# Two transformer blocks on one core: the order of the first pieces, of a two-tile group, and of the last products

## The chip, the cores and the metric

The kernel runs on one core of one Trainium2 chip. The metric is the device time in microseconds (us). Before the change it is 2211.89 us, the median of 3 runs (2210.44 to 2212.3). A core has TensorE (PE in the profile; its weight loads are PEld), VectorE (DVE), ScalarE (ACT), GpSimd (POOL) and SyncE (SP, whose queue issues nearly all DMAs here).

## The reference

A layer stack of two blocks over x of 256 tokens by 2048 channels, batch 1, all in float32. The first block:

```
h    = rms_norm(x, mix_norm_g)
proj = h @ w_in                                   # q, kv, gate logits, conv input
attn = nsa_attention(q, kv, sigmoid(gates), ...)  # 16 heads: compressed, selected, window branch
conv = silu(layer_norm(depthwise31(a * sigmoid(gate))))   # 1024 channels
x    = x + concat([attn, conv]) @ w_out
h    = rms_norm(x, ffn_norm_g)
x    = x + (silu(g) * a) @ w_down                 # g, a: halves of depthwise3(h @ w_up)
x    = rms_norm(x, final_norm_g)
```

The second block takes that x and computes MLA attention and gated linear attention side by side, both from one `w_in`, then an output projection and a gated feed-forward part, each between adaptive norms:

```
x = x + gate_m * rms_norm(concat([mla, gla]) @ w_out, g_post_mix)
h = rms_norm(x, g_pre_ffn) * (1 + scale_f) + shift_f
f = (silu(h @ w_gate) * (h @ w_up)) @ w_down
return x + gate_f * rms_norm(f, g_post_ffn)       # the kernel's last lines
```

## The kernel before

**Products.** Every float32 operand is split into a high and a low part, and a product is three matmuls that add up in one PSUM bank: high by high, low by high, high by low. The weights lie in DRAM in the order in which they are used, as a list of groups (`make_plan`, `GROUPS`). A group has its output tiles of 128 columns and is cut into pieces of 1024 weight columns (`MCS`), 24 matmuls of 128x256 each; the last groups (`g2_0` to `g2_3`, the second feed-forward's down projection) take the tokens as the stationary side, 12 matmuls of 128x512 a piece, half for tokens 0 to 127 (`ps[0]`) and half for 128 to 255 (`ps[1]`). `run_group` writes the products of one group; `next_mc` keeps the preparation of pieces ahead: ACT copies the high part (`split_h`, tile `wh`), DVE subtracts to get the low part (`split_l`, tile `wl`), and `load_raw` starts the next transfer of raw weights (`raw`, three buffers; two pieces a transfer but for the first four) on SP's queue.

**Block 1, first stage.** The rows of x come as `XT` (channels on partitions). For each 128 channels `feed_h` makes the high part of x times the norm's gain (ACT, tile `X`), `feed_l` the low part (DVE). The norm itself isn't needed for the products: 1/rms, called `R`, multiplies the results when they leave PSUM. So the groups of `w_in` run before R is there, and only their evacuation waits for it. `first_gen` feeds the rows, squares them (ACT), adds the squares up (DVE, tile `ss`), sums them over the channels on PE (`sums`, a product with ones, `vecs`) and takes the root (ACT) and the reciprocal (DVE, `R`).

**Attention and conv.** The groups of `w_in` are, in order, c0, c1, kvc, c2, kk, gt, q0, q1, c3, vv, q2, q3 (c: conv inputs, four tiles; q: queries, two tiles). `att_driver` starts the heads when the compressed keys, the keys and the gates are there. A head ends on DVE with the reciprocal of its row sums (`rs`), the multiplication by the gates and the weights `Pc`. `conv_gen` does the depthwise conv: 31 taps for 8 tiles of 128 channels are 240 multiply-adds on DVE (`cacc<-upad,cat,cacc`, the first tap is ACT's); then the layer norm over channels: an add (`upad<-upad,cacc`), sums on PE (`ps<-upad,vecs`, first sums), subtract and square, sums on PE (second sums), 1/std, multiply (`cacc<-cacc,R`), silu on ACT (`upad<-cacc,cat`), split into `ch` (ACT) and `cl` (DVE), by halves of 4 tiles. The output projection is in groups oa, ob (they read attention's output `o`, four heads' pairs each) and oz (reads `ch`, `cl`). The flag `conv0` is set after the first half, `conv1` after the second.

**What sets the order.** Each engine runs its instructions in the order in which the program was written, and a small planner writes it: `Clock` keeps an estimated time for each engine; `tick`, called between products, lets side work (generators such as `first_gen`, `conv_gen`) proceed when it is due; a side with `low=True`, only `conv_gen`, goes last and stops while the estimated DVE time runs ahead of PE's by more than a limit. `later` defers an evacuation. `halves` cuts the first piece in two halves of 512 columns. So a change of one group's place or of one engine's load reorders much of what follows. `finish` (line 1997) is the end of the kernel: for each half of the tokens the last square, the root, the gain, and four scalings with the residual, each followed by a DMA of 256 KB to the output.

The diagnostic line: all operations are issued by one helper, line 306, so the profile's rows are told apart by the tiles that they write and read.

Of the kernel before, what the change touches and what calls it, by code (L numbers as in the profile page):

```python
# [13 lines left out]
F32 = mybir.dt.float32  # L14
# [9 lines left out]
T = 256  # L24
# [16 lines left out]
def make_plan():  # L41
# [15 lines left out]
    conv(0)  # L57
    conv(1)
# [4 lines left out]
    q(0)  # L63
# [83 lines left out]
WARM = 8  # L147
SQ = 1
AHEAD = 2
SKIP = 48  # L150
# [223 lines left out]
class Kern:  # L374
    def __init__(self, nc, tc, a, dump=None, stop=None):
# [11 lines left out]
        self.hl = {}  # L387
# [60 lines left out]
    def load_raw(self, n):  # L448
        while self.loaded < min(n, MCS[self.last_mc]["tile"] + 1, self.used + RAW):
# [3 lines left out]
            self.sy.dma_start(raw[:, :L], bass.AP(tensor=w.tensor, offset=w.offset + off, ap=[[L, 128], [1, L]]))  # L453
# [3 lines left out]
    def split_h(self, i):  # L457
        m = MCS[i]
        h = self.wp.tile([128, 1024 + 64], F32R, name="wh", bufs=LA + 1)[:, OFF:]
        for a, b in halves(i, m["len"]):  # L460
            self.act(h[:, a:b], self.raws[m["tile"]][:, m["o"] + a:m["o"] + b], AF.Copy)
        self.hl[i] = h

    def split_l(self, i):
        m = MCS[i]
        n, h = m["len"], self.hl[i]
        l = self.wp.tile([128, 1024 + 64], F32R, name="wl", bufs=LA)[:, OFF:]
        for a, b in halves(i, n):
            self.tt(l[:, a:b], self.raws[m["tile"]][:, m["o"] + a:m["o"] + b], h[:, a:b].bitcast(F32), OP.subtract)
        self.hl[i] = (h, l)  # L470
        if i == len(MCS) - 1 or MCS[i + 1]["tile"] != m["tile"]:
            self.raws.pop(m["tile"])
            self.used = m["tile"] + 1
            self.load_raw(self.used + RAW)

# [76 lines left out]
    def run_group(self, g):  # L552
# [5 lines left out]
        src = self.src  # L558
# [10 lines left out]
        kl = len(g["ks"]) - 1  # L569
# [3 lines left out]
        for mi in g["mcs"]:  # L573
# [6 lines left out]
            h, l = self.next_mc(mi)  # L580
            t["PE"] = max(t["PE"], self.l_end.pop(mi))
            for u in range(nt if g["mode"] == "w" else 2):
                o = ps[u][:min(n, 128)] if g["mode"] == "w" else ps[u][:, :n]
                for q, k in enumerate(m["ks"]):
                    xh, xl = src(k, N)
                    if g["mode"] == "w":
                        c = slice(q * n + u * 128, q * n + u * 128 + min(n, 128))
                        p = ((h[:, c], xh), (h[:, c], xl), (l[:, c], xh))
                    else:
                        c, ts = slice(q * n, q * n + n), slice(u * 128, u * 128 + 128)  # L590
                        p = ((xh[:, ts], h[:, c]), (xl[:, ts], h[:, c]), (xh[:, ts], l[:, c]))
                    for i, (a, b) in enumerate(p):
                        self.mm(o[:, :b.shape[1]], a, b, k == 0 and i == 0, k == kl and i == 2)
# [3 lines left out]
            if mi != g["mcs"][-1]:  # L597
                self.tick()
# [1434 lines left out]
```

## Time and profile before

| | |
|---|---|
| median of 3 runs | 2211.89 us (2210.44 to 2212.3) |
| profiled execution, its own time | 2210.07 us |
| span of the profiled execution | 2208.1 us |
| mean granted clock of TensorE over the span | 0.996 of full speed |
| PE busy | 2176.1 us, 99% |
| DVE busy | 1695.1 us, 77% |
| ACT busy | 1187.3 us, 54% |
| chain that ended last | PE 92%, DVE 4%, ACT 2% |

The profile is of one execution. Busy time says how full an engine was over the whole span; the chain says what the end waited for, step by step. A row of the timeline gives the start in us from the span's start, the duration, the engine, the line, the operation with output and inputs, the shapes, and, in brackets, how long the engine had stood idle before it and on whose result. A row of a stretch gives busy time and count for PE, PEld, DVE, ACT and POOL, the granted clock (1.00 is 2.4 GHz, 0.50 is 1.2 GHz), the DMA share and the bytes moved per time.

### The profile page before, as it was taken

The page shows a single profiled execution, that of the slowest core. Times are in us where ns is not written, and L with a number is a line of the kernel's source. Part 1 is how long each engine was busy: PE and PEld are TensorE (multiplying, and loading weights), DVE is VectorE, ACT ScalarE, POOL GpSimd, SP SyncE. Part 2 cuts the span into 40 slices and gives each one's busy share as a digit, 9 for nine tenths or more (in the row PEclk, how much of TensorE's full clock was granted, in tenths as well). Part 3 has the DMA queues.
Part 4 walks back from the last instruction along what each step waited for, and adds up shares of the span by engine and source line. Part 5 has one row for each costly group of instructions (what it writes and reads, how often), then busy time and mean ns, then how long its engine had stood idle before and what let it go on. Part 6 is the DMA issues. An engine that isn't in the chain of part 4 may idle for free.

```text
span 2208.1 us, 42338 instructions
## 1 busy us (share of the span) xinstructions
PE 2176.1 (99%) x17486; PEld 2083.7 (94%) x17486; DVE 1695.1 (77%) x2632; ACT 1187.3 (54%) x1826; POOL 4.9 (0%) x16
## 2 busy tenths in 40 slices
PE   8999999999999999999999999999999999999997
PEld 8998889999999999999999889989998999899986
DVE  7998988999988799998879876678666665554455
ACT  5447786655553355555556664566444444444443
POOL 0000000000000000000000000000000000000000
PEclk9999999999999999999999999999999999999999
DMA  6544325688888887887756643546766765555553
GB/s 248 191 170 157 119 96 193 242 301 312 306 299 313 304 305 293 308 298 292 265 206 226 225 144 137 209 152 211 251 248 240 253 250 201 198 186 177 192 193 131
DMA packets 89089, 499.22 MB, mean 226 GB/s; under 512 B 9904, under 2 KB 12352, under 8 KB 42432
## 3 DMA queue, kind: packets, MB, share of 16 engines
q1 hardware_dynamic: 88896, 496.51, 62.8%
q8 instruction: 137, 2.24, 0.4%
q14 instruction: 56, 0.46, 0.1%
HBM read 494.35 MB, written 2.12 MB: 225 GB/s over the span
## 4 chain that ended last, share of the span: by engine, by line
PE 92%; DVE 4%; ACT 2%; issue 1%; DMA 1%; SPq 0%; DVEq 0%; ACTq 0%
PE ps L306 92%; DVE wl L306 1%; DMA raw<-in_wst_dram 1%; DVE cacc L306 1%; ACT wh L306 0%; DVE og L306 0%; ACT P L306 0%; DVE ss L306 0%; DVE XT L306 0%; DVE blk L306 0%; ACT L306 0%; ACT X L306 0%; DVE R L306 0%; DVE X L306 0%; DVE P L306 0%
## 5 line engine op out<-in xcount | busy, mean ns | idle before, releaser
L306 PE MATMUL ps<-X,wh 128*128 128x256 f32 (+1 forms) x7680 | 1333.1, 278 | 3.3 <-ACT X L306 2.6
L306 ACT ACTIVATE wh<-raw 128x1024 fp32r<-128x1024 f32 (+2 forms) x741 | 782.7, 1058 | 817.5 <-PE ps L306 770.8
L306 DVE TENSOR_TENSOR wl<-raw,wh 128x1024 fp32r<-128x1024 f32 (+2 forms) x741 | 897.8, 1215 | 404.8 <-PE ps L306 348.1
L306 PEld LDWEIGHTS ps<-X,wh 128*128 128x128 f32 x7680 | 1160.7, 188 | 11.9 <-issue 5.8
L306 PE MATMUL ps<-X,wl 128*128 128x256 f32 (+1 forms) x3840 | 1059.9, 276 | 3.5 <-DVE wl L306 3.5
L306 PEld LDWEIGHTS ps<-X,wl 128*128 128x128 f32 x3840 | 721.7, 188 | 4.5 <-DVE wl L306 4.5
L306 DVE SCALAR_TENSOR_TENSOR ac<-wa,cs,ac 128x512 f32<-128x512 f32 x360 | 269.4, 748 | 8.3 <-DMA wa<-in_wada_dram 2.0
L306 PE MATMUL ps<-hid,wh 128*128 128x256 f32 x1408 | 241.4, 276 | 0.0
L306 PE MATMUL ps<-wh,hid 128*128 128x512 f32 x704 | 216.7, 388 | 0.0
L306 PEld LDWEIGHTS ps<-hid,wh 128*128 128x128 f32 x1408 | 211.8, 188 | 1.2 <-issue 1.2
L306 PE MATMUL ps<-hid,wl 128*128 128x256 f32 x704 | 193.7, 275 | 0.0
L306 PEld LDWEIGHTS ps<-wh,hid 128*128 128x128 f32 x704 | 131.8, 188 | 27.4 <-issue 0.2
L306 PE MATMUL ps<-wl,hid 128*128 128x512 f32 x352 | 136.6, 388 | 0.0
L306 PEld LDWEIGHTS ps<-hid,wl 128*128 128x128 f32 x704 | 132.2, 188 | 0.0
L306 DVE SCALAR_TENSOR_TENSOR cacc<-upad,cat,cacc 128x256 f32<-128x256 f32 x240 | 99.6, 476 | 0.3 <-ACT cacc L306 0.2
L306 PEld LDWEIGHTS ps<-wl,hid 128*128 128x128 f32 x352 | 66.1, 188 | 13.6
L306 DVE SCALAR_TENSOR_TENSOR y<-vt,fv,y 128x256 f32<-128x256 f32 x176 | 73.3, 478 | 0.0
L306 PE MATMUL ps<-wh,X 128*128 128x512 f32 x192 | 61.1, 399 | 0.0
L306 ACT ACTIVATE y<-ps,fv 128x256 f32<-128x256 f32 x84 | 49.3, 587 | 0.0
L306 PE MATMUL ps<-o,wh 128*128 128x256 f32 x256 | 46.8, 283 | 1.2 <-ACT o L306 1.1
L306 ACT ACT_TABLE_LOAD x30 | 38.5, 1283 | 10.9 <-DMA XT<-in_x_dram 5.4
L306 PEld LDWEIGHTS ps<-wh,X 128*128 128x128 f32 x192 | 35.4, 188 | 6.7
(319 smaller groups left out, 1747.9 us busy)
## 6 DMA issues: line engine op xcount, KB each, us to landing
raw<-in_wst_dram SPq DMA_DIRECT2D x363, 1024.0 KB, 4.9
wa<-in_wada_dram SPq DMA_DIRECT2D x176, 512.0 KB, 6.2
wa<-in_wada_dram SPq DMA_DIRECT2D x32, 256.0 KB, 5.5
raw<-in_wst_dram SPq DMA_DIRECT2D x4, 768.0 KB, 4.3
raw<-in_wst_dram SPq DMA_DIRECT2D x4, 512.0 KB, 5.9
B<-dtab SPq DMA_DIRECT2D x8, 256.0 KB, 5.1
out_dram<-og SPq DMA_DIRECT2D x8, 256.0 KB, 2.8
XT<-in_x_dram SPq DMA_DIRECT2D x3, 512.0 KB, 7.1
```

The source lines that it names most:

```text
L306: return f(*x, **k)
```

## The change

1. **Group order.** q0, a two-tile group, comes second, behind c0, instead of behind gt.
2. **First piece.** `first_piece` does piece 0 in two halves of 512 columns, each with one row of x (`feed_h`, the half of `wh`, `feed_l`, the half of `wl`), and `run_group` writes its products row by row over all tiles instead of tile by tile. The first raw tile is loaded in two halves from ACT's queue, the next ones stay on SP's; XT's first two rows come in two transfers. One warm-up product fewer (`WARM` 7).
3. **Rows and squares.** `first_gen` feeds the rows of piece c when piece c-1 is prepared, and does all squares after all rows.
4. **Table.** An activation on a constant column (`kc[:, 4:5]`) is put ahead of the first use of XT, so that ACT's table is loaded there.
5. **End.** Of the last group's last three pieces (`TAIL`), half 0's products come first and half 1's after them (`held`, `products`). `last_add` takes each half in with two adds of 256 columns and squares of them, `last_scale` does the scalings; half 0's are done while half 1's products run, but for two.

```diff
@@ make_plan
     conv(0)
+    q(0)
     conv(1)
...
     add("gt", "w_in", [np.array([2560 + h * 3 + br for h in HORD for br in range(3)])], K16, 8)
-    q(0)
     q(1)
@@ constants
-WARM = 8
-SQ = 1
+WARM = 7
 AHEAD = 2
+TAIL = 3
@@ load_raw
-            self.sy.dma_start(raw[:, :L], bass.AP(tensor=w.tensor, offset=w.offset + off, ap=[[L, 128], [1, L]]))
+            for a, b in halves(self.loaded, L):
+                (eng or self.sy).dma_start(raw[:, a:b], bass.AP(tensor=w.tensor, offset=w.offset + off + a, ap=[[L, 128], [1, b - a]]))
@@ new
+    def first_piece(self, g):
+        h = self.wp.tile([128, 1024 + 64], F32R, name="wh", bufs=LA + 1)[:, OFF:]
+        l = self.wp.tile([128, 1024 + 64], F32R, name="wl", bufs=LA)[:, OFF:]
+        self.hl[0], raw = (h, l), self.raws[0]
+        for k, (a, b) in enumerate(halves(0, MCS[0]["len"])):
+            self.feed_h((k,), g)
+            self.act(h[:, a:b], raw[:, a:b], AF.Copy)
+            self.feed_l((k,), g)
+            self.tt(l[:, a:b], raw[:, a:b], h[:, a:b].bitcast(F32), OP.subtract)
+        self.prepped = 1
@@ run_group
+        ends = len(g["mcs"]) - (TAIL if g is GROUPS[-1] else 0)
...
+            us = range(nb)
+            if n_mc >= ends:
+                held.append((m, hl))
+                us = (0,)
+            order = [(u, q) for q in range(len(m["ks"])) for u in us] if mi == 0 else [(u, q) for u in us for q in range(len(m["ks"]))]
+            for u, q in order:
+                self.products(g, ps[u], u, m, q, hl, N)
...
+        if held:
+            self.later(lambda: self.last_add(0, ps[0]), False)
+            for m, hl in held:
+                for q in range(len(m["ks"])):
+                    self.products(g, ps[1], 1, m, q, hl, N)
+                    self.tick()
+            self.later(lambda: self.last_add(1, ps[1]), False)
+            self.flush()
+            return
@@ block1_setup
-        for n, (c0, c1) in enumerate(((0, 2), (2, 4), (4, 8))):
+        self.load_raw(1, nc.scalar)
+        for n, (c0, c1) in enumerate(((0, 1), (1, 2), (2, 4), (4, 8))):
             self.load_x(c0, c1)
-            self.load_raw(n + 1)
+            self.load_raw(n)
         self.load_x(8, 12)
+        self.act(self.kc[:, 4:5], self.eps, AF.Identity)
         g = lambda k: self.ca("mix_g", k)
-        self.feed_raw(range(2), g)
+        self.h_end[0] = self.clock.run(lambda: self.first_piece(g), 0.0)[1]
@@ first_gen
-        for c in range(1, 8 + SQ):
-            if c < 8:
-                self.feed_raw(range(2 * c, 2 * c + 2), g)
+        for c in range(1, 8):
+            while self.cur == "c0" and (self.prepped < c or self.emitted < c - AHEAD):
+                yield
+            self.feed_raw(range(2 * c, 2 * c + 2), g)
...
+        yield
+        ss4 = self.early.tile([128, 2, T], F32, name="ss4", tag="g1")
+        for c in range(8):
...
+            yield
@@ new, in place of finish
+    def last_add(self, tt, ps):
+        f = self.f[:, tt, 1536:]
+        q = self.f2.tile([128, 512], F32, name="q", tag="u")
+        for e in range(2):
+            c = slice(256 * e, 256 * e + 256)
+            self.tt(f[:, c], ps[:, c], f[:, c], OP.add)
+            self.act(q[:, c], f[:, c], AF.Square, accum_out=self.ssq[:, tt, 3 + e:4 + e])
+        self.last_f = self.f2.tile([128, 512], F32, name="lf", bufs=2), *getattr(self, "last_f", ())
+        self.tt(self.last_f[0], f, self.gpb[1][:, 1], OP.mult)
+        if tt:
+            self.last_scale(0, (2, 3), self.last_f[1])
+        R = self.rp.tile([128, T], F32, name="sd")[:, :1]
+        self.v.tensor_reduce(R, self.ssq[:, tt], axis=AX, op=OP.add)
+        self.act(R, R, AF.Sqrt, scale=1.0 / D, bias=self.eps)
+        r = self.rt[tt] = self.f2.tile([128, 1], F32, name="r", bufs=2)
+        self.v.reciprocal(r, R)
+        self.last_scale(tt, range(4) if tt else (0, 1), self.last_f[0])
```

The order of the instructions follows from the planner, so it is shown at three places.

VectorE at the start of the program, before (`X<-XT,cat,X` is the low part of a row, `wl` that of a piece, `ss<-ss,sq` the add of a square):

```order
L306 SCALAR_TENSOR_TENSOR X<-XT,cat,X 128x256 x2
L306 TENSOR_TENSOR wl<-raw,wh 128x512 x2
L306 SCALAR_TENSOR_TENSOR X<-XT,cat,X 128x256 x4
L306 TENSOR_TENSOR ss_154<-ss_154,sq_177 128x512
L306 TENSOR_TENSOR wl<-raw,wh 128x1024
L306 SCALAR_TENSOR_TENSOR X<-XT,cat,X 128x256 x2
L306 TENSOR_TENSOR ss_154<-ss_154,sq_204 128x512
L306 SCALAR_TENSOR_TENSOR X<-XT,cat,X 128x256 x2
L306 TENSOR_TENSOR ss_154<-ss_154,sq_229 128x512
L306 TENSOR_TENSOR wl<-raw,wh 128x1024 x2
```

The same place after the change:

```order
L306 SCALAR_TENSOR_TENSOR X<-XT,cat,X 128x256
L306 TENSOR_TENSOR wl<-raw,wh 128x512
L306 SCALAR_TENSOR_TENSOR X<-XT,cat,X 128x256
L306 TENSOR_TENSOR wl<-raw,wh 128x512
L306 SCALAR_TENSOR_TENSOR X<-XT,cat,X 128x256 x4
L306 TENSOR_TENSOR wl<-raw,wh 128x1024
L306 SCALAR_TENSOR_TENSOR X<-XT,cat,X 128x256 x2
L306 TENSOR_TENSOR wl<-raw,wh 128x1024 x2
L306 SCALAR_TENSOR_TENSOR X<-XT,cat,X 128x256 x4
L306 TENSOR_TENSOR wl<-raw,wh 128x1024 x2
L306 SCALAR_TENSOR_TENSOR X<-XT,cat,X 128x256 x2
L306 TENSOR_TENSOR wl<-raw,wh 128x1024
```

The adds of squares have gone from between the rows; they come after the last row, from the 17th instruction row on. On PE the sums of `ss` stand behind 240 products of `X` instead of 174.

VectorE at the end of attention, before, from the last head's `rs` on:

```order
L306 RECIPROCAL rs<-sm 128x6
L306 TENSOR_TENSOR rs<-rs,Gt 128x6
L306 SCALAR_TENSOR_TENSOR Pc_1829<-sc,rs,cat 128x16 x2
L306 TENSOR_TENSOR upad<-upad,cacc_91 128x2x256
L306 TENSOR_TENSOR o<-ps,o 128x256
L306 TENSOR_TENSOR wl<-raw,wh 128x1024
L306 TENSOR_TENSOR XT<-ps,XT 128x256 x4
L306 TENSOR_TENSOR cacc_90<-cacc_90,sd 128x1024
L306 TENSOR_TENSOR cacc_91<-cacc_91,sd 128x1024
```

The same place after the change:

```order
L306 RECIPROCAL rs<-sm 128x6
L306 TENSOR_TENSOR rs<-rs,Gt 128x6
L306 SCALAR_TENSOR_TENSOR Pc_1945<-sc,rs,cat 128x16 x2
L306 TENSOR_TENSOR XT<-ps,XT 128x256 x2
L306 SCALAR_TENSOR_TENSOR cacc_91<-upad,cat,cacc_91 128x256 x16
L306 TENSOR_TENSOR o<-ps,o 128x256
L306 TENSOR_TENSOR upad<-upad,cacc_91 128x2x256
L306 TENSOR_TENSOR wl<-raw,wh 128x1024
L306 TENSOR_TENSOR cacc_90<-cacc_90,sd 128x1024
```

Sixteen multiply-adds of the conv (`cacc_91<-upad,cat,cacc_91`) and two adds to XT now stand between the last `Pc` and the conv's last add (`upad<-upad,cacc_91`); there was nothing between them. The subtractions `cacc_90<-cacc_90,sd` belong to the norm behind the first sums.

TensorE at the conv's first sums (`ps<-upad,vecs`), before (`PT` are attention's last products, `o` the output projection):

```order
L306 MATMUL ps<-vecs,P_3721 128x128 x2
L306 MATMUL ps<-upad,vecs 128x256 x2
L306 MATMUL ps<-PT,vz 64x256 x2
L306 MATMUL ps<-PT,V 64x256 x2
L306 MATMUL ps<-PT,V 64x128 x2
L306 MATMUL ps<-PT,V 64x256 x2
L306 MATMUL ps<-PT,V 64x128 x2
L306 MATMUL ps<-o,wh 128x256 x2
L306 MATMUL ps<-o,wl 128x256
```

The same place after the change:

```order
L306 MATMUL ps<-PT,V 64x128 x2
L306 MATMUL ps<-PT,V 64x256 x2
L306 MATMUL ps<-PT,V 64x128 x2
L306 MATMUL ps<-o,wh 128x256 x2
L306 MATMUL ps<-o,wl 128x256
L306 MATMUL ps<-o,wh 128x256 x2
L306 MATMUL ps<-o,wl 128x256
L306 MATMUL ps<-upad,vecs 128x256 x2
L306 MATMUL ps<-o,wh 128x256 x2
L306 MATMUL ps<-o,wl 128x256
```

The first sums have moved behind the last products of attention and six of the output projection. Between the first and the second sums of the conv stood 18 products of `o`, and 174 between the second sums and the first product of oz (`ps<-ch,wh`); now it is 138 and 48.

## Rows read from the trace of the kernel before

**Rows 1.** The page, busy time of each engine and the chain that ended last
```profile
PE 2176.1 (99%) x17486; PEld 2083.7 (94%) x17486; DVE 1695.1 (77%) x2632; ACT 1187.3 (54%) x1826; POOL 4.9 (0%) x16
...
PE 92%; DVE 4%; ACT 2%; issue 1%; DMA 1%; SPq 0%; DVEq 0%; ACTq 0%
```

**Rows 2.** Timeline of PE at the start (start us, duration, instruction; wait before it)
```profile
8.13 0.51 PE L306 MATMUL ps<-X,wh 128*128 128x256 f32 x2 [0.73 <-ACT wh L306]
...
14.52 0.39 PE L306 MATMUL ps<-X,wl 128*128 128x256 f32 x1 [2.39 <-DVE wl L306]
...
18.45 0.39 PE L306 MATMUL ps<-X,wl 128*128 128x256 f32 x1 [0.90 <-DVE wl L306]
...
34.23 0.70 PE L306 MATMUL ps<-ss,vecs 128*128 128x256 f32 x2 [1.46 <-DVE ss L306]
```

**Rows 3.** Timeline of DVE in the last 20 us
```profile
2188.34 1.23 DVE L306 TENSOR_TENSOR wl<-raw,wh 128x1024 fp32r<-128x1024 f32 x1 [1.49 <-PE ps L306]
...
2196.44 0.69 DVE L306 TENSOR_TENSOR og<-ps,og 128x512 f32<-128x512 f32 x1 [0.67 <-PE ps L306]
...
2197.11 0.68 DVE L306 TENSOR_TENSOR og<-og,wa 128x512 f32<-128x512 f32 x1
...
2197.90 2.74 DVE L306 SCALAR_TENSOR_TENSOR og<-og,sd,XT 128x512 f32<-128x512 f32 x4
...
2200.56 0.15 DVE L306 TENSOR_REDUCE sd<-ssq 128x1 f32<-128x4 f32 x1
...
2201.41 2.74 DVE L306 SCALAR_TENSOR_TENSOR og<-og,sd,XT 128x512 f32<-128x512 f32 x4
```

**Rows 4.** Busy time by stretch, R to the conv's end, and oz
```profile
36.00:310.40 274.40, 271.34 (x2166) 250.64 (x2165) 250.16 (x643) 169.51 (x390) 0.57 (x2) 0.99 0.43 154
343.50:391.00 47.50, 47.14 (x416) 46.94 (x414) 41.31 (x70) 32.83 (x54) 0.14 (x2) 1.00 0.60 212
```

**Rows 5.** Timeline of PE, the conv's sums and the first oz product
```profile
313.91 1.03 PE L306 MATMUL ps<-upad,vecs 128*128 128x256 f32 x4
...
321.50 1.13 PE L306 MATMUL ps<-upad,vecs 128*128 128x256 f32 x4 [0.66 <-DVE upad L306]
...
343.51 0.28 PE L306 MATMUL ps<-ch,wh 128*128 128x256 f32 x1
```

**Rows 6.** Timeline of ACT and DVE at the start
```profile
5.36 1.28 ACT L306 ACT_TABLE_LOAD   x1 [5.36 <-DMA XT<-in_x_dram]
...
35.97 1.75 DVE L306 RECIPROCAL R<-sd 128x256 f32<-128x256 f32 x1 [0.20 <-ACT sd L306]
```

**Rows 7.** The page's groups, the conv's multiply-adds
```profile
L306 DVE SCALAR_TENSOR_TENSOR cacc<-upad,cat,cacc 128x256 f32<-128x256 f32 x240 | 99.6, 476 | 0.3 <-ACT cacc L306 0.2
```

**Rows 8.** Timeline of DVE at the end of attention
```profile
309.59 0.19 DVE L306 RECIPROCAL rs<-sm 128x6 f32<-128x6 f32 x1 [2.85 <-ACT sc L306]
...
310.38 0.68 DVE L306 TENSOR_TENSOR upad<-upad,cacc 128x512 f32<-128x512 f32 x1
...
313.34 1.41 DVE L306 TENSOR_TENSOR XT<-ps,XT 128x256 f32<-128x256 f32 x4
```

**Rows 9.** Timeline of ACT and DVE, from the conv's norm to its output
```profile
331.15 1.99 ACT L306 ACTIVATE wh<-raw 128x1024 fp32r<-128x1024 f32 x2
...
333.05 1.05 ACT L306 ACTIVATE ch<-upad 128x1024 fp32r<-128x1024 f32 x1
...
334.13 1.23 DVE L306 TENSOR_TENSOR cl<-upad,ch 128x1024 fp32r<-128x1024 f32 x1
...
335.27 1.22 DVE L306 TENSOR_TENSOR cacc<-cacc,R 128x1024 f32<-128x1024 f32 x1
...
336.52 2.08 ACT L306 ACTIVATE upad<-cacc,cat 128x256 f32<-128x256 f32 x4 [2.43 <-DVE cacc L306]
```

**Rows 10.** Busy time by stretch around the fall of the granted clock
```profile
1457.00:1460.30 3.30, 1.27 (x6) 0.68 (x4) 2.76 (x7) 1.17 (x3) 0.00 (x0) 1.00 0.74 293
1460.30:1467.10 6.80, 6.01 (x23) 5.25 (x24) 5.89 (x11) 4.11 (x9) 0.00 (x0) 0.50 0.00 0
```

More of the change, by code (lines that the diff above doesn't have):

```diff
@@ L459, in split_h @@
         h = self.wp.tile([128, 1024 + 64], F32R, name="wh", bufs=LA + 1)[:, OFF:]
-        for a, b in halves(i, m["len"]):
-            self.act(h[:, a:b], self.raws[m["tile"]][:, m["o"] + a:m["o"] + b], AF.Copy)
+        self.act(h[:, :m["len"]], self.raws[m["tile"]][:, m["o"]:m["o"] + m["len"]], AF.Copy)
         self.hl[i] = h
@@ L466, in split_l @@
         n, h = m["len"], self.hl[i]
[L467 to L470, printed above, removed]
+        if i:
+            l = self.wp.tile([128, 1024 + 64], F32R, name="wl", bufs=LA)[:, OFF:]
+            self.tt(l[:, :n], self.raws[m["tile"]][:, m["o"]:m["o"] + n], h[:, :n].bitcast(F32), OP.subtract)
+            self.hl[i] = (h, l)
         if i == len(MCS) - 1 or MCS[i + 1]["tile"] != m["tile"]:
@@ L579, in run_group @@
                 self.idle()
-            h, l = self.next_mc(mi)
+            hl = self.next_mc(mi)
             t["PE"] = max(t["PE"], self.l_end.pop(mi))
[L582 to L593, printed above, removed]
-                    if q % GRAN == GRAN - 1 and (u, k) != (nb - 1, m["ks"][-1]):
-                        self.tick()
+            us = range(nb)
[5 more added lines that the diff above has]
+                self.products(g, ps[u], u, m, q, hl, N)
+                if q % GRAN == GRAN - 1 and (u, m["ks"][q]) != (nb - 1, m["ks"][-1]):
+                    self.tick()
             self.emitted += 1
@@ L605, in run_group, with products @@
         self.tick()
+    def products(self, g, bank, u, m, q, hl, N):
+        n, (h, l), k = g["n"], hl, m["ks"][q]
+        xh, xl = self.src(k, N)
+        if g["mode"] == "w":
+            o = bank[:min(n, 128)]
+            c = slice(q * n + u * 128, q * n + u * 128 + min(n, 128))
+            p = ((h[:, c], xh), (h[:, c], xl), (l[:, c], xh))
+        else:
+            o = bank[:, :n]
+            c, ts = slice(q * n, q * n + n), slice(u * 128, u * 128 + 128)
+            p = ((xh[:, ts], h[:, c]), (xl[:, ts], h[:, c]), (xh[:, ts], l[:, c]))
+        for i, (a, b) in enumerate(p):
+            self.mm(o[:, :b.shape[1]], a, b, k == 0 and i == 0, k == len(g["ks"]) - 1 and i == 2)
     def xsrc(self, k, N=T):
@@ new lines, in last_scale @@
+    def last_scale(self, tt, js, last):
+        x = self.XT.rearrange("p (c a) t -> p c (a t)", a=2)
+        for j in js:
+            o = self.f[:, tt, 512 * j:512 * j + 512]
+            f = last if j == 3 else o
+            self.stt(o.rearrange("p (c n) -> p c n", c=2), f.rearrange("p (c n) -> p c n", c=2), self.rt[tt],
+                     x[:, 2 * j:2 * j + 2, 256 * tt:256 * tt + 256], OP.mult, OP.add)
+            self.sy.dma_start(self.a["out"][128 * tt:128 * tt + 128, 512 * j:512 * j + 512], o)
```

43 lines of the change are left out of this document (10 added, 33 removed).

## The prediction

> **What bounds the kernel now.** I read the busy shares and the chain first: TensorE is busy 99% of the span and 92% of the chain that ended last is its products [rows 1]. So an edit pays only where PE stands still, and the next view is the idle time at PE's own rows. At the beginning it stands 0.73 us for the first weights, 2.39 and 0.90 us for `wl` of the second and third pieces and 1.46 us for the sum of squares `ss` [rows 2]: 5.5 us in all. At the end the span of 2208.1 runs on for 11.7 us after the last product, on VectorE, whose last add starts at 2196.44 [rows 3]. In between, the table by stage (columns: stretch, PE, PEld, DVE, ACT, POOL busy, granted clock, DMA share, GB/s) shows that from 36 to 310 us PE is full but DVE works 250.2 of 274.4 us as well [rows 4]: attention and the depthwise conv of block 1 live there. Their end is due on PE: the conv's first sums start at 313.91 with no wait, its second ones at 321.50 after 0.66 us, and the oz products that read the conv's output at 343.51 with no wait [rows 5]. That is a schedule with nothing to spare, and it hangs on R, which is ready from 35.97 + 1.75 us [rows 6]. The change moves R.
>
> **The beginning.** One piece is 24 products. A stretch of nothing but products gives 47.14 / 416 = 0.113 us each [rows 4], so 2.72 us a piece.
> Gains: piece 0 is split and multiplied row by row, with one warm-up product fewer and the table load moved ahead of the XT transfer (1.28 us, which now ends the wait for XT [rows 6]). First product about 0.9 us earlier (the most is the 1.28). `wl` of the second piece stood behind four row subtractions and a square's add on DVE; in the new order it stands behind the rows but no add, and its raw tile lands no sooner. I take 1.1 of the 2.39 us and all of the 0.90 us [rows 2], and charge 0.7 for a new wait at the fifth piece, whose `wl` now stands behind four rows. Net 2.2 us; the bounds are 0 and 0.9 + 3.3 = 4.2.
> Cost: all squares now come after all rows, so the sums of `ss` stand on PE behind 240 products instead of 174. 66 x 0.113 = 7.5 us, less the 2.2 gained, less the 1.46 us wait for `ss` that goes [rows 2]: R is 3.8 us later (bounds 1.8 and 7.5). No evacuation of the first groups can run before R, so glu, attention and conv all start that much later. q0 second costs two banks and no product; what it could give is an earlier start of attention, below.
>
> **From R to the conv's sums.** On DVE the work between R and the conv's last add is the same but for some 0.8 us (the same instructions, with five more). If DVE idles as much as before (274.4 - 250.2 = 24.2 us [rows 4]), the last add of the conv comes 3.8 + 0.8 = 4.6 us later, and the first sums at 313.91 + 4.6 = 318.5 [rows 5]. The order gives a second reading: 16 of the conv's multiply-adds, of 99.6 / 240 = 0.415 us [rows 7], now stand after the last head's `rs`, where none stood. With `rs` at 309.59 as before, 0.8 to the end of Pc (310.38), 0.7 for two XT adds (1.41 for four), 16 x 0.415 = 6.6, 0.35 for an o add (as one XT add), 0.68 for the conv's add [rows 8], and 0.2 to PE's start, the sums stand at 319.0; `rs` itself could be later by R's delay. The two agree; I take 319.0, with bounds 313.9 (attention, freed by the early q0, cuts the idling by as much as R is late) and 322 (R 7.5 us late). PE reaches that point earlier than before and waits, which is where the gain of the beginning is spent: below it counts for nothing.
> From there PE's order decides. Before, 18 o products stood between the two sums; now 138. The second sums come at 319.0 + 1.03 + 138 x 0.113 = 335.7 instead of 321.50 [rows 5]. From them to `ch` of the first half took 12.6 us (321.50 to 333.05 + 1.05), in which two `wh` of 1.99 us stood ahead of `ch`; these have gone from that place, so 10.6 [rows 9]: oz starts at 346.3 rather than 343.51. The cover is gone too: only 48 o products (5.4 us) are left behind the second sums, 335.7 + 1.1 + 5.4 = 342.2, so PE waits 4.1 us. Then comes a wait that was hidden before: the second half of the conv. After `ch` at 346.3, `cl` 1.23, the product with R 1.22, four silu 2.08, a `wh` 1.0, `ch` 1.05 and `cl` 1.2 [rows 9] end at 354.0 (rounded), where before the second piece could go on at 343.51 + 2.72 = 346.2. That is 7.7 us with what is rounded; I take **7.6**, bounds 0 and 11. Behind the waiting oz product stand all later ones, and PE is 99% busy after it [rows 4], so it isn't won back.
>
> **TensorE's clock.** In one place of this trace PE stood 2 us beside thin work (1.27 of 3.30 us busy) and the granted clock was then 0.50, the 1.2 GHz level, for 6.80 us [rows 10]; after the 2.39 us wait at the start it didn't fall. Waits of 4 us in front of oz lie beyond both. A fall of the length seen costs 6.01 us of busy time at half rate, 3.0; the shortest that I could defend is nothing. I take 1.7, near the middle, once.
> The Trainium skill (TensorE: Matmul & The Clock Gate, section "HAM oscillation — how this bites in real kernels") says that a loop whose waits re-throttle the array pays again at each wait. This trace bears it out at one of the two places; with a payment at each of the two long waits before oz the sum would be 1.7 us higher, which is the third rival.
>
> **The end.** The last three pieces do half 0's products first, so half 0 is complete 18 products of 512 columns before the end (18 x 2 x 0.113 = 4.1 us), and half 1 at the same time as now. Before, the last add stood at 2196.44, a multiply of 0.68 follows, then four scalings of 2.74 for half 0, and half 1's four from 2201.41 to 2204.15 [rows 3]. After: two adds of half width 0.7 from 2196.44, the multiply 0.68, half 0's last two scalings 1.37, then reduction, root and reciprocal 0.85 (2201.41 less 2200.56 before), four scalings 2.74: 2202.8. That is **-1.4** (bounds -2.5 and 0). `wl` of the last piece, which waited for its buffer 1.49 us [rows 3], gets it when the piece four earlier is done, 8.2 us before the end, and is ready 6.8 before it; half 0 of the last piece wants it 5.0 before it (4.1 + 4 products): nothing lost.
>
> **Sum.** On the profiled execution of 2210.1: +7.6 - 1.4 + 1.7 = 2218.0. The median of the runs stands 1.8 above that execution: **2219.8 us**.
>
> **Rivals.**
> *Attention catches up.* The early q0 lets the heads start when gt is done instead of 10.9 us later (four pieces), so DVE idles less than its 24.2 us [rows 4]. For it: those us of idling are there; against: the conv is given low priority and the order still leaves 16 of it to the end. With 3.5 us less idling the sums come at 315.5, oz loses 4.1 instead of 7.6, no clock fall: 2210.1 + 4.1 - 1.4 + 1.8 = 2214.6.
> *The other side: the conv is in time.* If DVE idles some 7 us less, the conv's last add is there by 311 and PE never waits at the sums. PE keeps 2.2 + 1.46 = 3.7 of the beginning and 1.4 of the end: 2210.1 - 5.1 + 1.8 = 2206.8. It decides from a last add of about 311 on; the 16 multiply-adds after `rs` would have to start before 304, against which the order speaks.
> *The clock falls at both waits.* 2219.8 + 1.7, and as much again if a fall stretches the conv's chain: 2221.5 to 2223.2.
> *The beginning doesn't gain.* The first raw tile is issued from ACT's queue, behind nothing, but its halves share the transfers with XT. If piece 0 is no earlier, R is 2.2 later, the sums at 321: 2222.
>
> **How the numbers follow.** Forecast 0.44 (own range 2217 to 2222.5), attention catches up 0.24, the conv in time 0.14, the clock falls twice 0.12, no gain at the start 0.06. What a measurement can tell from no change is 0.2%, 4.4 us: below 2207.5 or above 2216.3. Faster: 0.12 of the 0.14. Same: 0.02 of it, 0.20 of the catching up and 0.02 of the forecast, 0.24. Slower: the rest, 0.64. The range from 2208.5 to 2224.5 leaves out some 0.12 below and 0.05 above.
>
> **What would show it.** In the profile of the changed kernel: the first product near 7.2 and the sums of `ss` near 38.0 with no wait; R near 39.8; the conv's first sums at 318.5 to 320 with a wait of 3 us or more in front; the second ones with no wait; oz with a wait of about 4 us on `ch` and another, of some 4 in parts, on the second half; the granted clock at 0.50 for a few us right there; the last scaling 1.4 us nearer to PE's last product. A conv sum before 314, or an oz without a wait, proves the forecast wrong, and a time under 2210 does so too.

## The result and the profile after

The changed kernel takes 2223.53 us (median of 4 runs, 2222.85 to 2225.03) against 2211.40 of the kernel before beside it: ratio 1.0058, 95% interval 1.0046 to 1.0071. It is slower by 12 us, on the side that was forecast (+7.9), 4 us more than the likeliest case and 1.0 above that case's own range (2217 to 2222.5). The profiled execution took 2224.05.

The page of the changed kernel, busy time and the chain that ended last:

```profile
PE 2181.7 (98%) x17484; PEld 2088.2 (94%) x17484; DVE 1697.4 (76%) x2634; ACT 1187.5 (53%) x1829; POOL 4.9 (0%) x16
...
PE 90%; DVE 4%; ACT 4%; DMA 1%; issue 1%; DVEq 0%; ACTq 0%
```

PE's share of the chain fell from 92 to 90% and ACT's rose from 2 to 4%, while DVE's stayed at 4% [rows 1]: on the path to the end PE now waits for ACT more often.

PE and DVE at the start of the changed kernel, and the stretch in which the clock fell (columns of the stretch: length, PE, PEld, DVE, ACT, POOL busy, granted clock, DMA share, GB/s):

```profile
6.07 0.50 PE L306 MATMUL ps<-X,wh 128*128 128x256 f32 x2
...
10.76 0.50 PE L306 MATMUL ps<-X,wh 128*128 128x256 f32 x2 [1.18 <-ACT wh L306]
...
13.55 0.39 PE L306 MATMUL ps<-X,wl 128*128 128x256 f32 x1 [2.28 <-DVE wl L306]
...
40.23 0.70 PE L306 MATMUL ps<-ss,vecs 128*128 128x256 f32 x2
...
41.97 1.75 DVE L306 RECIPROCAL R<-sd 128x256 f32<-128x256 f32 x1 [0.20 <-ACT sd L306]
```
```profile
14.80:18.10 3.30, 3.30 (x18) 3.30 (x17) 1.95 (x2) 1.06 (x1) 0.00 (x0) 0.50 0.89 344
```

The first product comes 2.1 us earlier than before (8.13 [rows 2]), but PE then stands 1.18 us for the second piece's `wh` and 2.28 us for its `wl`, and runs at the 1.2 GHz level for 3.3 us. The sums of `ss` stand at 40.23 instead of 34.23 and R at 41.97 instead of 35.97 [rows 6]: 6.0 us late, in these two executions.

PE in the middle of the changed kernel: a product of attention, the conv's first and second sums, the two halves of the conv in front of oz, and the sums behind oz:

```profile
278.40 0.69 PE L306 MATMUL ps<-PT,vz 128*64 128x256 f32 x1 [3.19 <-ACT PT L306]
...
326.76 1.10 PE L306 MATMUL ps<-upad,vecs 128*128 128x256 f32 x4 [2.66 <-DVE upad L306]
...
343.36 1.03 PE L306 MATMUL ps<-upad,vecs 128*128 128x256 f32 x4
...
354.19 0.58 PE L306 MATMUL ps<-ch,wh 128*128 128x256 f32 x1 [4.34 <-ACT ch L306]
...
355.45 0.58 PE L306 MATMUL ps<-cl,wh 128*128 128x256 f32 x1 [0.68 <-DVE cl L306]
...
360.59 0.38 PE L306 MATMUL ps<-ch,wh 128*128 128x256 f32 x1 [0.36 <-ACT ch L306]
...
361.85 0.39 PE L306 MATMUL ps<-cl,wh 128*128 128x256 f32 x1 [0.88 <-DVE cl L306]
...
406.89 0.70 PE L306 MATMUL ps<-ss,vecs 128*128 128x256 f32 x2 [0.63 <-DVE ss L306]
```

The first sums wait 2.66 us and are 12.9 us later than before, the first oz product waits 4.34 us and is 10.7 us later [rows 5], and the sums behind oz, at 391.27 before, are 15.6 us later. From there nothing more is lost: PE's last product ends 15.7 us later than before (2212.1 against 2196.4), and the end gives 1.5 us of it back. DVE at the end of attention shows the queue that the forecast read from the order:

```profile
317.80 0.18 DVE L306 RECIPROCAL rs<-sm 128x6 f32<-128x6 f32 x1
...
319.27 6.42 DVE L306 SCALAR_TENSOR_TENSOR cacc<-upad,cat,cacc 128x256 f32<-128x256 f32 x16
...
325.94 0.68 DVE L306 TENSOR_TENSOR upad<-upad,cacc 128x512 f32<-128x512 f32 x1
```

Sixteen multiply-adds take 6.42 us between the last head and the conv's last add; before, 0.8 us lay between `rs` and that add [rows 8]. But `rs` itself is 8.2 us late.

The clock around the two long waits of the changed kernel:

```profile
275.00:278.40 3.40, 0.21 (x1) 0.00 (x1) 2.31 (x15) 2.88 (x12) 0.00 (x0) 0.88 0.00 0
278.40:282.00 3.60, 3.60 (x18) 2.32 (x18) 0.67 (x5) 3.08 (x14) 0.00 (x0) 0.50 0.00 0
...
350.00:354.20 4.20, 0.01 (x1) 0.01 (x1) 1.63 (x4) 3.13 (x5) 0.00 (x0) 0.82 0.76 250
354.20:358.00 3.80, 3.12 (x13) 2.83 (x14) 3.47 (x3) 1.43 (x3) 0.00 (x0) 0.50 0.03 6
```

In front of both PE did almost nothing (0.21 of 3.40 us, 0.01 of 4.20), and behind both the granted clock is 0.50, as at [rows 10]. Behind the 2.66 us wait at 326.76 it stayed at 1.00.

A ledger makes the kernels comparable. From stretches of 2 us between 0 and 420, idle is the stretch less PE's busy time, and half rate is the busy time times (1 - granted clock):

| kernel | median us | ratio to before, 95% | idle | half rate | sum |
|---|---|---|---|---|---|
| before | 2211 | | 13.2 | 1.7 | 14.9 |
| changed | 2223.5 | 1.0046 to 1.0071 | 23.3 | 8.7 | 32.0 |
| e1 squares early | 2212.4 | 0.9999 to 1.0016 | 13.7 | 6.6 | 20.3 |
| e2 q0 second only | 2222.8 | 1.0043 to 1.0069 | 22.0 | 7.7 | 29.7 |
| e3 q0 back | 2212.8 | 0.9999 to 1.0017 | 13.5 | 6.7 | 20.2 |
| e4 end only | 2209.1 | 0.9984 to 1.0002 | 10.9 | 4.7 | 15.6 |
| e5 changed, limit 1.5 | 2217.7 | 1.0018 to 1.0041 | 16.6 | 8.3 | 24.9 |
| e6 before, limit 2.0 | 2221.1 | 1.0032 to 1.0060 | 19.7 | 5.9 | 25.6 |
| e7 both undone | 2206.9 | 0.9974 to 0.9991 | 11.4 | 3.3 | 14.7 |
| e8 changed, filled wait | 2225.8 | 1.0055 to 1.0083 | 19.0 | 9.5 | 28.5 |
| e9 e1, R late | 2219.5 | 1.0022 to 1.0050 | 18.1 | 7.4 | 25.5 |
| e10 end, early table | 2209.1 | 0.9982 to 0.9999 | 13.3 | 4.9 | 18.2 |

Idle and half rate of the changed kernel are 17.1 us above those of before: 10.1 of standing still and 7.0 of half rate. The 1.5 of the end go the other way; the rest, 15.6, is 1.6 more than the 14.0 between the two profiled executions, and what makes up these 1.6 stays open. (e8's idle leaves out the 3.6 us of its filler.) Each row is one execution. Before and e4 run the same instructions in the same order up to 420, and they differ by 2.3 in idle and by 3.0 in half rate, in the sum by 0.7: so a column that differs by 3 us between two kernels says little by itself.

### The profile page after: what moved, and what is told of

It is laid out like the page before. It is cut to its first block, busy times and chain, and to the rows that moved or that the text cites. A ratio compares the mean times of both kernels' runs of the same rounds, so it can differ in the third digit from the quotient of the medians.

```text
span 2222.2 us, 42343 instructions
## 1 busy us (share of the span) xinstructions
PE 2181.7 (98%) x17484; PEld 2088.2 (94%) x17484; DVE 1697.4 (76%) x2634; ACT 1187.5 (53%) x1829; POOL 4.9 (0%) x16
## 4 chain that ended last, share of the span: by engine, by line
PE 90%; DVE 4%; ACT 4%; DMA 1%; issue 1%; DVEq 0%; ACTq 0%
PE ps L306 90%; ACT P L306 1%; DVE wl L306 1%; DVE cacc L306 1%; DMA raw<-in_wst_dram 1%; ACT wh L306 1%; DVE blk L306 0%; ACT L306 0%; DMA B<-dtab 0%; ACT sc L306 0%; DVE XT L306 0%; ACT PT L306 0%; DVE P L306 0%; DVE rs L306 0%; DVE og L306 0%
## 5 line engine op out<-in xcount | busy, mean ns | idle before, releaser
L306 PE MATMUL ps<-X,wh 128*128 128x256 f32 (+2 forms) x7680 | 1334.7, 278 | 3.7 <-ACT X L306 2.6
L306 PEld LDWEIGHTS ps<-X,wh 128*128 128x128 f32 (+1 forms) x7680 | 1162.2, 188 | 12.5 <-issue 5.8
L306 PE MATMUL ps<-X,wl 128*128 128x256 f32 (+2 forms) x3840 | 1060.4, 276 | 2.8 <-DVE wl L306 2.7
L306 PEld LDWEIGHTS ps<-X,wl 128*128 128x128 f32 (+1 forms) x3840 | 722.2, 188 | 3.6 <-DVE wl L306 3.6
L306 PE MATMUL ps<-ch,wh 128*128 128x256 f32 x128 | 36.5, 285 | 4.7 <-ACT ch L306 4.7
```

Of the source, the lines that this page charges most:

```text
L306: return f(*x, **k)
```

## The experiments

Theory A: the squares behind all rows make R late, and that is what everything behind it pays. Theory B: q0 in second place costs by itself. After the first four runs a third was added, C: what costs is the order that the planner writes.

**e1, squares beside their rows again** (the rest as changed; `first_gen` in short):

```diff
-        for c in range(1, 8):
-            while self.cur == "c0" and (self.prepped < c or self.emitted < c - AHEAD):
-                yield
+        for c in range(1, 9):
+            if c < 8:
+                while self.cur == "c0" and (self.prepped < c or self.emitted < c - AHEAD):
+                    yield
...
+            x = self.XT[:, 2 * c - 2:2 * c]
+            if c == 1:
                 self.act(ss4, x, AF.Square)
...
```

> The changed kernel, with one part undone: each square is taken and added one step behind its rows again, q0 stays second, the end stays new. Theory A (the squares behind all rows make R late, and the lateness is what attention, conv and oz pay for): R's reciprocal starts before 38.5 instead of 41.97, the conv's first sums stand with a wait under 1.5 us, the two waits on the conv's output in front of oz (4.3 and some 2 us in parts) are gone, and so are the falls of the clock behind the 3.2 and 4.3 us waits. Time 2209 to 2212, 0.995 to 1.000 of the kernel before. Theory B (q0 in second place reshuffles attention and conv whatever R does): the waits in front of the first conv sums and of oz stay at 2.5 us or more each, and the time is 2218 or more.

2212.44 us. PE of e1 at the conv's first sums:

```profile
316.69 1.13 PE L306 MATMUL ps<-upad,vecs 128*128 128x256 f32 x4 [0.76 <-DVE upad L306]
```

R starts at 37.36, and this wait is 0.76 us instead of 2.66; those in front of oz are gone. B's 2218 falls; A's upper end, 2212, is missed by 0.4. The falls of the clock behind the 3.2 and 4.3 us waits are gone; the ledger's 6.6 us of half rate lie elsewhere, 1.6 or 1.7 of it each near 14, 51, 188 and 324.

**e2, q0 second and nothing else**, in the kernel before:

```diff
     conv(0)
+    q(0)
     conv(1)
...
-    q(0)
     q(1)
```

> The kernel before with one edit: q0 is the second group. Theory A: R comes later by little, since squares stay beside their rows (35.97 before, up to 38), so attention and conv are nearly in time: 2211 to 2216, at most one wait of over 3 us before 345. Theory B: the whole loss, 2219 or more, with waits of 4 us in front of oz.

2222.83 us: B's number, and A misses. R starts at 37.05, no later than in e1. The loss sits in two waits for attention's `PT`, not in front of oz:

```profile
286.83 0.69 PE L306 MATMUL ps<-PT,vz 128*64 128x256 f32 x1 [5.62 <-ACT PT L306]
...
330.61 0.69 PE L306 MATMUL ps<-PT,vz 128*64 128x256 f32 x1 [3.07 <-ACT PT L306]
```
```profile
280.00:286.80 6.80, 1.21 (x8) 0.62 (x6) 2.65 (x9) 6.80 (x29) 0.00 (x0) 0.93 0.47 154
286.80:292.00 5.20, 5.17 (x26) 3.89 (x27) 5.18 (x13) 3.58 (x8) 0.00 (x0) 0.50 0.01 3
```

PE works 1.21 of 6.80 us and then runs at half rate. With q0 second in both and R alike (37.05, 37.36), e1 and e2 are 10.4 us apart, of which the new end, which e2 lacks, makes 2 (e4): neither q0's place nor R's lateness alone sets the time. That is where theory C came from.

**e3, q0 back behind gt**, squares still late (in the changed kernel, the four lines of e2 reversed):

> The changed kernel with q0 back behind gt; squares still after all rows. Theory A: R is still late (41 to 42), and now the four-tile groups run out of banks while they wait for R, so that PE stands for 3 to 5 us near 37 to 40 us; the conv then is as late as R against PE's own place, no more: time 2212 to 2216. Theory B: the loss goes with q0, 2208 to 2211.

2212.84 us, as A expected, though R is less late than it said: 39.92, not 41 to 42. PE of e3 at the sums of `ss`:

```profile
37.76 0.82 PE L306 MATMUL ps<-ss,vecs 128*128 128x256 f32 x2 [4.19 <-DVE ss L306]
```

It stands 4.19 us for `ss`: without a two-tile group in second place PE has no banks left for another group while R is missing (`run_group` asks for four). Beside e7 below, which differs in the squares alone, R is 3.6 us late (39.92 against 36.29) and the conv's first sums are 4.8 us late (316.90 against 312.11, each with the same wait of 0.76).

**e4, the new end alone** (`TAIL`, `products`, `last_add`, `last_scale` in the kernel before):

> The kernel before with the new end alone (last three pieces by halves of the tokens, adds by 256 columns, scalings of half 0 while half 1 runs). Both theories: 1.4 to 2.0 us faster (the last scaling ended 7.7 us after PE's last products before, 5.9 in the changed kernel): 2209.4 to 2210.0, nothing else moved. Against it: if wl of the last piece is late for the held order, PE would wait some 0.5 us there and the gain would be 1 us.

2209.13 us, 2.0 below, as expected, though the interval of the ratio just reaches 1.

**e5, the changed kernel with the conv's limit at 1.5 us:**

```diff
-LAG = 1.0
+LAG = 1.5
```

> The changed kernel with one number of the planner changed: the low-priority conv may be written when DVE is planned up to 1.5 us ahead of PE, not 1.0. Nothing of the change is undone: q0 is second, the squares come late, R will again stand at 42. In the order four conv multiply-adds instead of sixteen are left behind the last head's rs. Theory C (what costs is the order written for attention and conv, not q0's place nor R as such): the waits on the conv in front of oz and the wait on PT near 278 us shrink below 2 us each, with the clock's falls behind them, and the time is 2209 to 2214. Theory B (q0 second costs by itself): 2219 or more. Theory A (R late costs by itself): the last add of the conv is as late as in the changed kernel within 2 us, 2217 or more.

2217.68 us: half of what was to come back (5.9 of 12), under B's number, above C's and 0.7 inside A's. But A's sign isn't there: the last add of the conv starts at 318.99, 7 us earlier than in the changed kernel (325.94), not within 2. So none of the three has it whole. The waits in front of oz and the one near 278 are gone; others stand in their place:

```profile
294.28 0.43 PE L306 MATMUL ps<-PT,vz 128*64 128x256 f32 x1 [2.87 <-ACT PT L306]
...
318.99 0.48 PE L306 MATMUL ps<-vecs,Pc 128*128 128x128 f32 x2 [3.47 <-DVE Pc L306]
```

**e6, the kernel before with that limit at 2.0:**

> The kernel before with that limit at 2.0 us, nothing else: q0, the rows and the end as before. Theory C: the order is reshuffled too and no longer fits; new waits of 2 to 4 us on attention's results in the stretch from 270 to 330 us, with a fall of the clock behind some of them: 2214 to 2221, with R at 36. Theories A and B, by which nothing in the change touches this kernel: 2211, as before, or better since the conv is done sooner.

2221.05 us, 10 us slower, at the upper end of C's range. Nothing of the change is in it, and R stands at 37.15, where e4, with the start of before as well, has it at 36.60:

```profile
279.04 0.69 PE L306 MATMUL ps<-PT,vz 128*64 128x256 f32 x1 [3.48 <-ACT PT L306]
...
316.69 0.43 PE L306 MATMUL ps<-PT,vz 128*64 128x256 f32 x1 [3.12 <-ACT PT L306]
```
```profile
278.00:282.00 4.00, 2.96 (x16) 2.09 (x17) 1.07 (x10) 3.81 (x16) 0.00 (x0) 0.50 0.02 4
```

The same two kinds of waits as in e2, with the same fall behind the first. So an order that fits badly costs nearly as much as the whole change, without a late R and with q0 in its old place.

**e7, both undone** (q0 behind gt as in e3, squares as in e1; first piece, table and end as changed):

> The changed kernel with both undone that touch the middle: q0 behind gt, squares beside their rows; the first piece row by row, the early table and the new end stay. Theory A and C: R before 37, waits as in the kernel before, PE's gain of the start kept if the clock doesn't fall there: 2208 to 2210. If the start's gain is absorbed by the waits of 1 us each before the conv's second sums: 2209.5 to 2211, the end's gain alone.

2206.86 us, 0.9974 to 0.9991 of before: the fastest of all, faster than both kernels and below both ranges that were expected. PE and DVE of e7:

```profile
14.23 0.58 PE L306 MATMUL ps<-X,wl 128*128 128x256 f32 x1 [2.96 <-DVE wl L306]
...
36.29 1.75 DVE L306 RECIPROCAL R<-sd 128x256 f32<-128x256 f32 x1 [0.20 <-ACT sd L306]
...
312.11 1.13 PE L306 MATMUL ps<-upad,vecs 128*128 128x256 f32 x4 [0.76 <-DVE upad L306]
```

R is no earlier than before, though 1.8 us of the conv's way are gained (312.11 against 313.91 [rows 5]), and the end gives its 2 us.

**e8, the wait in front of oz filled** with eight products of constants, in the changed kernel:

```diff
     def pre_oz0(self):
+        o = self.bank()
+        for _ in range(8):
+            self.pe.eng.matmul(o[:, :T], self.ones, self.vecs[:, :T], start=True, stop=True)
+        self.free(o)
```

> The changed kernel with eight idle products of constants (fp32, 128x256, about 0.5 us each) on PE between the last product of o and the first of oz, where PE stood still for 4.3 us and ran at half rate after it. They write a bank that nobody reads. Theory on the clock (the fall follows the standing still): the granted clock stays at 1.00 in 354 to 362 us, the 2.3 us lost at half rate there are gone, the wait in front of oz is under 1 us, and the total is 1 to 2.5 us below the changed kernel's: 2221 to 2222.5. Rival (the fall doesn't hang on the wait): clock 0.5 again, total 2223.5 or more.

2225.75 us: no gain; the time is on the rival's side. PE of e8, the filler, the first oz product and the one that reads the second half, and the clock:

```profile
350.54 3.62 PE L1253 MATMUL ps<-vecs 128*128 128x256 f32 x16
355.04 0.39 PE L306 MATMUL ps<-ch,wh 128*128 128x256 f32 x1 [0.88 <-ACT ch L306]
...
362.69 0.39 PE L306 MATMUL ps<-cl,wh 128*128 128x256 f32 x1 [0.88 <-DVE cl L306]
```
```profile
354.20:358.00 3.80, 2.09 (x14) 1.89 (x15) 2.98 (x3) 1.37 (x3) 0.00 (x0) 0.95 0.02 2
358.00:362.00 4.00, 2.91 (x13) 2.42 (x12) 1.10 (x2) 4.00 (x7) 0.00 (x0) 0.62 0.01 2
```

The wait is 0.88 us and the clock holds to 357.6, which agrees with the first half of the expectation; then it falls all the same (357.58 on), and the second half of the conv is there at 362.69, not earlier than at 361.85 without the filler. From the first oz product to that one it is 7.65 us with the filler and 7.66 without, though the ledger has 1.2 us of half rate there instead of 2.3. What ended that stretch was the conv's chain on ACT and DVE (from 358 to 362 ACT is busy 4.00 of 4.00 us), so half rate there had cost nothing. Why e8 is 2 us slower than the changed kernel is shown only in part: its clock also fell behind the 2.66 us wait, and its second sums stand 18.2 us behind the first ones instead of 16.6.

**e9, R late in e1's order.** Seven adds of 0.68 us on a tile that is no longer needed, ahead of R and unknown to the planner, so that every engine's order is e1's:

```diff
         self.v.reciprocal(self.Rt, self.Rt)
+        for _ in range(7):
+            self.v.eng.tensor_tensor(ss4, ss4, ss4, op=OP.add)
         self.R = self.rstd(o, D)
```

> The kernel of e1 (the changed one with the squares beside their rows, 2212.4) with seven adds of 0.68 us on ss4, a tile that nothing needs any more, on DVE in front of R's reciprocal; the planner isn't told of them, so that every engine's order is e1's, and R stands at 41 to 42.5 as in the changed kernel. Theory A (R late costs by itself): waits on the conv or on PT of 3 us and more as in the changed kernel, 2218 or more. Theory C (the order that the planner writes for a late R costs): the delay is taken up by DVE's idle time before attention, the waits grow by under 2 us in sum beside e1, 2212 to 2215.

2219.46 us (2216.7 to 2222.0): A's number. DVE and PE of e9:

```profile
42.72 1.74 DVE L306 RECIPROCAL R<-sd 128x256 f32<-128x256 f32 x1
```
```profile
48.27 0.39 PE L306 MATMUL ps<-X,wl 128*128 128x256 f32 x1 [3.85 <-DVE wl L306]
...
322.47 1.13 PE L306 MATMUL ps<-upad,vecs 128*128 128x256 f32 x4 [0.76 <-DVE upad L306]
```

R is 5.4 us later than in e1, and PE pays at once: it stands 3.85 us for a `wl` that is queued on DVE behind the first results that need R. The conv's first sums come 5.8 us later than in e1, with the same wait of 0.76. So DVE's idle time took up nothing of the delay; C's expectation fails here. So do A's signs: no wait of 3 us on the conv or on `PT` is there, and most of what is paid is paid at 48 us. The adds also keep DVE itself busy (five us from 37.78), so the run shows what five us cost when DVE loses them in front of attention; a late R without that is in e3.

**e10, end and early table** (one line, `self.act(self.kc[:, 4:5], self.eps, AF.Identity)`, added to e4):

> The kernel of e4 (before with the new end, 2209.1) with the early table load added, and nothing else of the start. By the forecast's step the first product comes 0.7 to 1.3 us earlier, 7.0 to 7.4; but wl of the second piece stands where it stood, so PE waits that much longer there (3 us or more rather than 2.4) and the total stays 2208.5 to 2210. Rival: the table is what the start's gain of e7 (2206.9) came from: 2207 to 2208, with wl of the second piece early as well.

2209.07 us, as e4. PE of e10:

```profile
7.28 0.50 PE L307 MATMUL ps<-X,wh 128*128 128x256 f32 x2 [0.70 <-ACT wh L307]
...
14.15 0.39 PE L307 MATMUL ps<-X,wl 128*128 128x256 f32 x1 [2.86 <-DVE wl L307]
```

The first product comes 0.85 us earlier than before, where XT landed at the same time (ACT's wait for it ends at 5.40 here, at 5.36 before; in e4 it ended at 4.49, and the first product stood at 7.33 with the table late). The next wait is 2.86 instead of 2.39 us [rows 2], so 0.4 us of the 0.85 are left after it; the sums of `ss`, which wait for DVE, stand no earlier for it, and none of it shows in the time.

## Why the prediction was right, and where it was short

The side and the path were right: R late, the conv late behind it, PE waiting in front of oz. That the number came within 4 us owes something to luck. From profile to profile the change cost 14.0 us where 7.9 were forecast (+7.6 - 1.4 + 1.7); the medians are nearer because the forecast added 1.8 us to the profiled execution of before, while the changed kernel's median lies 0.5 below its own. The term that was too small is the 7.6: the second half of the conv is read 15.6 us later than before (361.85 against 346.2).

**The two edits that cost.** e7, e1, e3 and the changed kernel differ only in q0's place and the squares' place:

| | q0 behind gt | q0 second |
|---|---|---|
| squares beside their rows | 2206.9 | 2212.4 |
| squares behind all rows | 2212.8 | 2223.5 |

Late squares cost 6.0 us, q0 second 5.6, and both together 5.1 more than their sum (each median against a before of 2210.7 to 2211.4 beside it; e1's runs spread from 2209.2 to 2214.8, so the figures are good to 1 or 2 us). These are prices in this kernel and not of the edits as such: q0 second alone costs 11.7 in the kernel before (e2). What goes with the 5.1 is the order: in the other three cells 38 products stand between the conv's two sums and 174 in front of oz, as before; with both edits 138 and 48 do. e5 has both edits and the old 38 and 174, and it costs 10.8 above e7, about the sum without the 5.1. The forecast named the first and the waits that they draw; the price of q0 second it set at nothing, and as a rival even below.

**The beginning.** "Net 2.2 us" for PE failed: the first product came earlier than forecast (6.07, not 7.2), but the wait for the second piece's `wl` kept 2.28 of 2.39 us and a new one of 1.18 us for its `wh` stands ahead of it, and the half rate behind them took 1.7 us (3.30 x 0.5). So the 7.5 us of extra products in front of the sums were offset by the 1.5 of the wait for `ss` alone: R was 6.0 us late, not 3.8, inside the bounds (1.8 to 7.5). Part of this is the execution's and not the kernel's: e5 and e8 have the same instructions up to there, their first products stand at 6.79 and 6.76, the 1.18 us wait isn't there, and R stands at 40.72 and 41.07; with the start of before, e4 and e6 have R at 36.60 and 37.15. By these, R is 3.6 to 6.0 late. In the changed kernel's execution ACT stood 1.03 us for XT and 0.77 for raw weights before that `wh`. The fall at the start isn't the change's own: e4, with the start of before, shows 2.8 us of half rate in its first 20 us, where the profiled execution of before shows none.

**Late R.** That the delay is handed on whole to attention and conv ("if DVE idles as much as before") is shown by e3 beside e7 (3.6 us in, 4.8 out, with 23.9 us of idle DVE) and by e9 beside e1 (5.4 in, 5.8 out, with the adds' own time on DVE).

**From R to the conv's sums.** Here the forecast was 7.8 us short (319.0 against 326.76, beyond its bound of 322). Two steps failed. In its first reading it is "If DVE idles as much as before". DVE from R to the conv's last add in the changed kernel:

```profile
42.00:325.96 283.96, 273.56 (x2157) 250.45 (x2155) 251.85 (x648) 171.21 (x397) 0.57 (x2) 0.98 0.42 146
```

It idled 32.1 us (283.96 - 251.85), not 24.2 [rows 4], and worked 1.7 more, not 0.8. So the last add came 15.6 us later (6.0 of R, 1.7 and 7.9), where 4.6 were forecast. That reading also moved the sums by the whole 4.6, though before the last add had ended 2.85 us ahead of them (311.06 and 313.91 [rows 5, 8]); by its own terms they would stand at 315.9, and that it agreed with the second reading was chance. In the second reading it is "With `rs` at 309.59 as before", which the forecast itself called open: `rs` stood at 317.80. Behind it, the sixteen multiply-adds were right (6.42 us for 6.6). The heads did not come evenly later: the twelfth `rs` stood at 281.19, 3.2 us earlier than before (284.40), the thirteenth at 297.09, 5.1 later than before (292.04). Just ahead of the twelfth lies the wait on `PT` at 278.40 (3.19 us), with 3.0 us of half rate around it (0.8 and 2.2 in the ledger's stretches of 260 to 280 and 280 to 300). Behind it lies a block of the conv. DVE's time on the conv's multiply-adds from the tenth `rs` to the twelfth and from there to the thirteenth (columns: stretch, DVE busy, granted clock, DMA share, GB/s), before:

```profile
270.80:284.40 13.60, 3.32 (x8) 1.00 0.23 78
284.40:292.04 7.64, 3.24 (x8) 1.00 0.51 174
```

The same in the changed kernel:

```profile
270.70:281.19 10.49, 0.00 (x0) 0.83 0.29 115
281.19:297.09 15.90, 6.58 (x16) 0.90 0.25 85
```

Two heads follow each other with nothing of the conv between them, and the next one has sixteen in front of it. The forecast didn't see this, because it looked only at the three places where it showed the order. e2 and e6 have the same sixteen at that place and a like wait on `PT`, with R near 37; e1, e3 and e7 have eight, as before, and no such wait: it comes of the order. Whether the bunching itself draws the wait, and why the planner writes it, was not tried.

**The second sums and oz.** 138 products between the sums: forecast 16.7 us, measured 343.36 - 326.76 = 16.6. From them to oz 10.8 (10.6). The wait 4.34 us (4.1). The second half is read at 361.85, 7.7 after the first oz product (7.7). This chain was right step by step; it only began later. One sign in it was not: the waits for the second half are 1.9 us in parts (0.68, 0.36, 0.88), not 4, since PE did its products there at half rate.

**The clock.** "I take 1.7, once", in front of oz. There was a fall there (half rate for 2.3 us in the ledger), but e8 shows that it cost nothing. Those at 278 and at the start stand where PE was working without a wait; what each cost was not tried apart. The rule of the Trainium skill (TensorE: Matmul & The Clock Gate, section "HAM oscillation — how this bites in real kernels"), by which each such wait pays again, agrees as to the falls with three places (1.18 + 2.28 us at the start, 3.19, 4.34), not with the 2.66 us one. As to the price, the 4.34 us one cost nothing, because there PE was not what was waited for.

**The end.** Forecast -1.4, by the profile -1.5: from PE's last product to the end of the last scaling it took 7.7 us before (2196.4 to 2204.15) and takes 6.2 now (2212.1 to 2218.34; the 5.9 of e4's expectation was misread):

```profile
2212.16 0.76 DVE L306 TENSOR_TENSOR og<-ps,og 128x256 f32<-128x256 f32 x2 [0.48 <-PE ps L306]
...
2217.59 0.75 DVE L306 SCALAR_TENSOR_TENSOR og<-lf,r,XT 128x512 f32<-128x512 f32 x1
```

e4 measured 2.0.

**The rivals.** "Attention catches up" had the sign wrong. q0 second does not let the heads start sooner: it pushes kvc, kk and gt back by a group, and the heads wait for gt. Some 50 more products of `X` stand on PE ahead of the first `rs` for it: 1399 products in all in the changed kernel, 1350 before. The first `rs` stood at 168.84 before, 173.89 in the changed kernel, and 175.12 in e1 with an R that was 1.4 us late. "The conv in time" didn't come about here; e7 shows what it is worth (2206.9, forecast 2206.8), with the two edits undone. "The beginning doesn't gain" (0.06) had R right in the profiled pair, 2.2 us later than forecast, but for another reason (piece 0 was 2.1 us earlier), and its sums at 321 were 5.8 us short. "The clock falls at both waits" (0.12) comes nearest with its number, 2221.5 to 2223.2, and by luck: behind the wait in front of the first sums the clock stayed at 1.00, and the fall in front of oz cost nothing.

**What stays open.** In e1, q0 second costs 5.6 us beside e7: the ledger has waits of 1.5 and 2.2 us on a transfer of weights (`w`) and on a head's P near 108 and 187, and two falls of 1.6 to 1.7 more than e7. The ledger's sums differ by as much as the times (20.3 and 14.7); why the waits stand there wasn't tried apart.

## What to carry to other kernels

Where two engines are both near their limit, the result that everything waits for (here R) is worth more than the first product: trace each moved instruction to it, and charge the delay whole. In a program whose order a planner writes, a moved group or one changed limit rewrites the order hundreds of us later, so read the order of the whole stretch up to the next point where the engines meet, not only at the edited places; here a limit alone (e6) cost 10 us, nearly as much as the change. Test the parts of a bundle apart: of this one the start without its late squares and the end gave 4 us together (e7), and two others took 17 with what they do to each other.

## What the runs showed of the hardware that was not expected

The fall of the clock comes and goes for the same code: 0.0 us of half rate in the first 20 us of before, 2.8 in e4, whose start is the same. The wait in front of the conv's first sums is 2.66 us in the changed kernel and in e8, with the same products around it; behind it the granted clock was 1.00 in the one and 0.61 (326 to 330) in the other, and e8's second sums came 1.6 us later behind its first ones. And a wait filled with idle products (e8) held the clock at 1.00 for 7 us, until 357.6, after which it fell behind two waits of 0.88 us.

A fall also came where PE did not wait. In the kernel before, PE ran thirty small products (33x128 by 33x16) without standing still, and the clock was then at the 1.2 GHz level for 3.4 us:

```profile
46.53 3.52 PE L306 MATMUL ps<-cat,oht 33*128 33x16 f32 x30
```
```profile
50.60:54.00 3.40, 3.40 (x19) 3.40 (x18) 2.00 (x6) 0.00 (x0) 0.00 (x0) 0.50 0.67 236
```

All twelve kernels have such a fall there, beginning during these products or within 1.4 us after them. The prediction's passage on the clock looked only at waits and doesn't have it.
